# Fillers of a sparse-attention stage: a second pair of tiles for rope, another order, another share per slot

## The chip, the cores and the metric

The kernel runs on one core of a Trainium2 chip. The time is the device time of one execution in microseconds (us). Before the change the median of three runs is 815.24 us, the lowest 814.93, the highest 816.38. In the rows of the profile PE is TensorE's matmuls, PEld its weight loads, DVE VectorE, ACT ScalarE, POOL GpSimd and SP SyncE, which issues most DMAs. A letter q behind an engine's name means its sequencer.

## What is computed

One layer of a decoder on 512 tokens of width 1024, all in float32. The part that matters here, from the reference, shortened:

```
proj = h @ w_in                       # u, q, kc, vc, ks, vs, kw, vw, g_nsa, g_merge
q  = apply_rope(q)                    # 16 heads of 64
k_cmp, v_cmp = compress(kc), compress(vc)
for each block of queries:
    o_c = softmax(q k_cmp) v_cmp      # compressed branch
    o_s = softmax(q k_sel) v_sel      # selected blocks; with 8 blocks all are taken
    o_w = softmax(q k_win) v_win      # window of 512, so all earlier tokens
    o   = gate0*o_c + gate1*o_s + gate2*o_w
merged = sig(ga) * (y_pool @ w_proj_pool) + sig(gb) * (y_nsa @ w_proj_nsa)
x = x + merged @ w_out
x = x + square(relu(rms(x) @ w_ff1)) @ w_ff2
```

Rope turns each half of a head's 64 numbers against the other: `x*cos + swap(x)*sin`, where swap exchanges the halves.

## The kernel before, in words

Every product of two float32 operands is made of three matmuls of rounded halves (high times high, high times low, low times high), so a weight tile is first split into `wh` (ACT, line 351) and `wl` (DVE or POOL, line 353). A projection of 128 output channels takes 24 matmuls of 128x128 by 512 (line 394).

**The stages.** First come the normalization and most projections (`P1`, line 125), up to about 182 us; then attention, up to about 390 us; then output projections and an MLP that is worked by sums of quarter matrices, up to the end. Thirteen projections are left over from the first stage and serve as **fillers** of the attention stage (`FILL2`, line 127): `gb0` to `gb7` are gate columns whose result ACT copies to `GB`, and `q3` to `q7` are queries of head pairs 3 to 7. A filler is cut into four steps of six matmuls. After the thirteen, four more steps start the projection `pn0`, so there are 56 steps.

**Attention** runs over 96 slots, twelve for each of eight head pairs (line 988). Iteration i of the loop (line 1132) emits the scores of slot i+1 (`score_pe`, two matmuls, line 1013), the transposes of slot i-4 (`turn_pe`, line 1075), mask and minimum of slot i on DVE (`smax`, line 1035), the exponential on ACT (line 1045), the weights of slot i-1 on POOL (`weight`, line 1058), the split of the transposed block on ACT and DVE (lines 1086, 1090), and each second time the product with V (line 1109). Then come one step of each side generator (`step_side`, line 1157) and the fillers' share. At slot 3 of each pair a side generator starts the compressed branch of the next pair (`cmp_scores`, line 945; its DVE instruction at line 962 subtracts a minimum from `cw`, both in SBUF). The output of a pair is put into plane p of `oT` by DVE (line 1118).

**Rope of a query** (`rope`, line 612) is a side generator too. ACT copies the projection to `rx` (618), four DMAs on SP's queue swap its quarters into `rs` (621), POOL multiplies both by cosine and sine in halves of 128x256 (626, 629), DVE adds them (634), and then `q_done` makes `Q` of it (659 to 664). There is one pair of tiles `rx`, `rs`. The count `scored["rope"]` stands at 1 while a rope is under way, to the very end, and the filler generator gives up its turn before a `q` filler as long as it does (line 897). A rope of query i also holds its last part back until `scored["pairs"]` is i-2 (line 635), since only three tiles `Q` exist.

**The share.** After slot i the count of steps that are done is to be at least `done0 + (total - done0) * (i + 1) // 102` (line 1158), where `done0` is what was done before slot 0; the loop fills until it is there or the generator gives up. For i below 5 one step more is tried (line 1161).

**What sets the order.** The program calls are emitted as above, and a scheduler then places each engine's instructions, mostly in the order of their emission; each engine works through its own queue in order. POOL and SP also issue the DMAs that add quarters of the MLP's weights in DRAM ahead of time (`add_sum`, line 273; `make_sum`, line 265), and SP the weight loads (line 235).

Of the kernel before, what the change touches and what calls it, by code (L numbers as in the profile page):

```python
# [13 lines left out]
F32 = mybir.dt.float32  # L14
# [6 lines left out]
S = 512  # L21
# [6 lines left out]
LAG, PLAG = 4, 2  # L28
# [34 lines left out]
def trunk(ctx: ExitStack, tc: tile.TileContext, A, out):  # L63
# [4 lines left out]
    def pool(name, **kw):  # L68
        return tc.tile_pool(name=name, bufs=1, reuse_waits="tile", **kw)
# [35 lines left out]
    def add_key(k):  # L105
        i = int(k[-1]) if k[-1].isdigit() else None
        if k in IN_COLS:
            add_cols(k, w_in, IN_COLS[k])
        elif k[:2] in ("wk", "wv"):
            w = A["w_c" + k[1] + "1"][0]  # L110
            add_w(k, [(w[512 * i:512 * i + 512, :].rearrange("(k p) c -> p k c", p=128), 0)])
        elif k[0] == "V":
            k0, k1 = ((0, 3), (3, 6), (6, 8))[i]
            wv = w_in[k0 * 128:k1 * 128, :].rearrange("(k p) c -> p k c", p=128)
            add_w(k, [(wv[:, :, 1920:2048], 0), (wv[:, :, 2176:2352], 128)])
        elif k == "wpool":
            add_w(k, [(w_pool.rearrange("g c d -> c g d"), 0)])
        elif k[:2] == "pp":
            add_w(k, [(w_pp[:, 256 * i:256 * i + 256].rearrange("(k p) c -> p k c", p=128), 0)])
        else:  # L120
            c0 = {"u": 0, "q": 512, "ga": 2352, "gb": 3376}[k[:-1]]
            add_cols(k, w_in, c0 + 128 * i)
# [1 line left out]
    IN_COLS = {"ck": 1536, "cv": 1664, "ks": 1792, "kw": 2048}  # L124
    P1 = ("ck ks u0 wk0 wk1 u1 wk2 u2 kw wk3 cv V0 V1 V2 wv0 u3 wv1 q0 wv2 wpool ga0 ga1 wv3 ga2 q1 "
          "ga3 ga4 ga5 q2 ga6 ga7 pp0 pp1 pp2 pp3").split()
    FILL2 = "gb0 q3 q4 q5 gb1 gb2 q6 gb3 q7 gb4 gb5 gb6 gb7".split()
    for k in P1 + FILL2:
        add_key(k)
    for j in range(8):  # L130
# [85 lines left out]
    def emit_load():  # L216
# [20 lines left out]
        if sums_after(i):  # L237
            make_sum(began)
        if i >= len(P1) + len(FILL2) + 4 and (len(begun) > 2 or begun and st["sums"] == len(jobs)):
            add_sum()  # L240
        return True

    def sums_after(i):

        if i < MLP0:
            return len(P1) + 3 <= i < len(P1) + len(FILL2) + 8
        return i % 3 == 0
# [10 lines left out]
    def make_sum(load):  # L258

        if st["sums"] < len(jobs):  # L260
            to, q, _ = jobs[st["sums"]]
            while any(q is jobs[n][0] for n in begun):
                add_sum()
            with tc.issue_after(load.ins):
                nc.sync.dma_start(to, q)
            begun.append(st["sums"])
            st["sums"] += 1

    def add_sum(behind=None):

        to, _, q = jobs[begun.popleft()]
        with tc.issue_after(behind.ins) if behind else nullcontext():
            POOL.dma_start(to, q, accum_op=ALU.add)  # L273

    part = {}
    mode = {"pool": False, "first": POOL}
# [185 lines left out]
    def fm(key, psp, post, xT=hT, sub=0, nk=8):  # L462

        wH, wL = use(key) if isinstance(key, str) else key
        ps = psp.tile([128, S], F32, tag="F", bufs=f_banks[0], name="psF")
        yield from pieces(ps, fm_products(wH, wL, xT, sub, nk))
        r = post(ps)
        if r is not None:
            next(r)
            side.append(r)  # L470
# [9 lines left out]
    oT = op.tile([128, 8, S], F32, name="oT")  # L480
    oTf = oT.rearrange("p j t -> p (j t)")
    at = ExitStack()
    ap = at.enter_context(pool("att"))
# [124 lines left out]

    scored = {"pairs": 0, "rope": 0}
    last_exp = []  # L610

    def rope(ps, scale, done, after=0):

        assert not scored["rope"]
        scored["rope"] = 1
        xr = ap.tile([128, S], F32, tag="rx", bufs=1, name="rx")
        sw = ap.tile([128, S], F32, tag="rs", bufs=1, name="rs")
        ACT.activation(xr, ps, AF.Copy, scale=scale)
        for b in range(4):
            a = b ^ 1  # L620
            nc.sync.dma_start(sw[32 * b:32 * b + 32, :], xr[32 * a:32 * a + 32, :])
        yield
        eng = POOL if mode["pool"] else DVE
        hs = [slice(0, S // 2), slice(S // 2, S)]
        for c in hs:
            eng.tensor_tensor(xr[:, c], xr[:, c], cosT[:, c], op=ALU.mult)
            yield
        for c in hs:
            eng.tensor_tensor(sw[:, c], sw[:, c], sinT[:, c], op=ALU.mult)
            yield  # L630
        yield
        for c in hs:
            yield
            DVE.tensor_tensor(xr[:, c], xr[:, c], sw[:, c], op=ALU.add)
        while scored["pairs"] < after:
            yield
        for _ in done(xr):
            yield
        scored["rope"] = 0

    def k_done(br):
        def done(k):
# [13 lines left out]
    def q_done(p):  # L656
        def done(q):
            t = ap.tile([128, 2, S], FR, tag="Q", bufs=3, name="Q")
            ACT.activation(t[0:64, 0, :], q[0:64, :], AF.Copy)
            ACT.activation(t[64:128, 1, :], q[64:128, :], AF.Copy)  # L660
            yield
            DVE.tensor_tensor(t[64:128, 0, :], q[0:64, :], t[0:64, 0, :].bitcast(F32), op=ALU.subtract)
            yield
            DVE.tensor_tensor(t[0:64, 1, :], q[64:128, :], t[64:128, 1, :].bitcast(F32), op=ALU.subtract)
            Q[p] = t
        return done

    with ExitStack() as c1:
# [184 lines left out]
        for k in P1[2:]:  # L853
            i = int(k[-1]) if k[-1].isdigit() else None
# [35 lines left out]
    with ExitStack() as c2:  # L890
        p2 = c2.enter_context(pool("p2"))
        ps2 = c2.enter_context(pool("ps2", space=PSUM))
        def fill2():
            for k in FILL2:
                i = int(k[-1])
                if k[0] == "q":
                    while scored["rope"]:
                        yield True
                    post = (lambda i: lambda ps: rope(ps, 1.0, q_done(i), i - 2))(i)
                else:  # L900
                    def post(ps, i=i):
                        ACT.activation(GB[:, i, :], ps, AF.Copy)
                yield from fm(k, ps2, post)
            free.append(True)
            split_ready()
            early[0] = use("pn0") + (ps2.tile([128, S], F32, tag="F", bufs=F_BANKS, name="psF"),)
            for k in range(7):
                while (k, 1) not in split:
                    yield True
                proj_k(early[0], k)  # L910
                if k % 2 or k == 6:
                    ahead()
                    yield
# [4 lines left out]
        def split_ready():  # L918

            while free and ready:  # L920
                p, half = ready.pop(0)
                c = slice(256 * half, 256 * half + 256)
                ACT.activation(OT[0][:, p, c], oT[:, p, c], AF.Copy)
                DVE.tensor_tensor(OT[1][:, p, c], oT[:, p, c], OT[0][:, p, c].bitcast(F32), op=ALU.subtract)
                split.add((p, half))

        def proj_k(w, k):
            mms(w[2], split_products(w[0][:, k, :], w[1][:, k, :], OT[0][:, k, :], OT[1][:, k, :]),
                first=k == 0, last=k == 7)
# [6 lines left out]
        def fill(n=1):  # L936
            for _ in range(n):
                if next(filler, True):
                    return False
                fdone[0] += 1  # L940
            return True
# [185 lines left out]
        n = len(slots)  # L1127
        total = 4 * len(FILL2) + 4
        done0 = fdone[0]
        after = deque()  # L1130
        score_pe(0)
        for i in range(n + LAG + PLAG):
            if i < n:
                p = slots[i][0]
                if i % 12 == 3 and p + 1 < NPAIR:
                    while p + 1 not in Q:
                        fill()
                        step_side()
                if i % 12 == CMP_AT and p + 1 < NPAIR:
                    side.append(cmp_scores(p + 1))  # L1140
            if i + 1 < n:
                score_pe(i + 1)
                scored["pairs"] = (i + 2) // 12
            t = i - LAG
            if 0 <= t < n:
                turn_pe(t)
                turn_hi(t)
            if i < n:
                smax(i)
                expo(i)  # L1150
            if 0 <= i - 1 < n:
                last = weight(i - 1)
            if i % 4 == 3 and len(begun) > 1:
                add_sum(last)
            if 0 <= t < n:
                turn_lo(t)
            step_side()
            want = done0 + (total - done0) * (i + 1) // (n + LAG + PLAG)
            while fdone[0] < want and fill():
                pass  # L1160
            if i < 5:
                fill()
            j = t - PLAG
            if 0 <= j < n and j % 2 == 1 and pv(j):
                o_evac(*slots[j][0:2])
# [99 lines left out]
    with ExitStack() as c3:  # L1265
        q3 = c3.enter_context(pool("q3"))
# [339 lines left out]
    for t in (2, 3):  # L1606
        n = 512 if t == 2 else 256
# [44 lines left out]
```

## Time and profile before

| what | value |
|---|---|
| median of the runs | 815.24 us |
| the profiled execution | 814.65 us |
| its span, first to last instruction | 812.9 us |
| mean granted TensorE clock | 0.994 |
| busy PE, DVE, ACT, POOL | 788.6, 627.4, 491.6, 207.8 us |

The profile is of one execution; outside its span lie 1.75 us. A matmul that is issued with pauses is drawn longer than its pitch, so a busy PE is not always a PE at its peak, and PEclk, the granted share of the TensorE clock, has to be read beside it. In a table of windows each row gives, for each engine, the busy time and, in brackets, the instructions that overlap the window.

### The profile page before, as it was taken

What the parts mean: (1) busy time and instruction counts of PE and PEld (TensorE: products, weight loads), DVE (VectorE), ACT (ScalarE), POOL (GpSimd) and SP (SyncE); (2) the same over time, 40 slices, a digit from 0 to 9 for tenths busy, and PEclk for the clock granted to TensorE, in tenths of its full rate; (3) what the DMA queues carried; (4) which work ended last, traced back from release to release, by engine and by line L of the source; (5) the groups of instructions that cost most, each with busy time, mean ns of one, the idle gap of its engine ahead of it and who ended that gap; (6) DMA issues with size and microseconds to landing.
All of it is one profiled execution on the core that took longest, in us unless ns stands there. A gap on an engine that the chain in (4) does not pass through costs nothing.

```text
span 812.9 us, 14154 instructions
## 1 busy us (share of the span) xinstructions
PE 788.6 (97%) x5163; PEld 710.2 (87%) x5163; DVE 627.4 (77%) x1217; ACT 491.6 (60%) x968; POOL 207.8 (26%) x273
## 2 busy tenths in 40 slices
PE   8999999998899999999999999999999999999996
PEld 7889878886788888888788899999999999999996
DVE  5796744539879898889664579996889688978975
ACT  6576533337777888899434466943773477347833
POOL 4000000028766867665334100111111110000000
PEclk9999999999999999999999999999999999999999
DMA  9554633357446634553964707999998997754522
GB/s 304 143 158 122 164 92 94 102 170 153 67 124 122 144 79 92 104 131 65 328 152 154 202 9 208 311 243 283 250 286 218 285 266 194 222 164 156 181 79 104
DMA packets 128752, 136.65 MB, mean 168 GB/s; under 512 B 5349, under 2 KB 117001, under 8 KB 128522
## 3 DMA queue, kind: packets, MB, share of 16 engines
q1 hardware_dynamic: 107274, 113.98, 43.5%
q0 software_dynamic: 21120, 20.97, 18.1%
q8 instruction: 41, 0.67, 0.3%
q10 hardware_dynamic: 288, 0.79, 0.3%
q14 instruction: 29, 0.24, 0.1%
HBM read 131.01 MB, written 44.04 MB: 215 GB/s over the span
## 4 chain that ended last, share of the span: by engine, by line
PE 73%; DVE 16%; ACT 6%; issue 3%; DMA 1%; POOL 1%; ACTq 0%; DVEq 0%; POOLq 0%
PE psF L394 22%; PE psB L1379 15%; PE psB L394 12%; PE psB L1498 9%; PE psO L1109 3%; PE psT L1075 3%; PE psS L1013 2%; DVE wl L308 2%; PE psV L394 2%; DVE P L1035 2%; DVE PT L1090 1%; PE psF L451 1%; ACT P L1045 1%; DVE w3l L308 1%; PE psC L714 1%
## 5 line engine op out<-in xcount | busy, mean ns | idle before, releaser
L394 PE MATMUL psF<-R,wh 128*128 128x512 f32 x512 | 166.8, 404 | 0.9 <-ACT GB L688 0.6
L306 ACT ACTIVATE wh<-raw 128x1024 fp32r<-128x1024 f32 x70 | 74.0, 1057 | 74.5 <-PE psB L1498 32.6
L351 ACT ACTIVATE wh<-raw 128x512 fp32r<-128x512 f32 (+1 forms) x100 | 60.2, 620 | 82.2 <-PE psF L394 37.4
L394 PEld LDWEIGHTS psF<-R,wh 128*128 128x128 f32 x512 | 92.5, 189 | 18.7 <-ACT GB L688 0.8
L273 POOL DMA_DIRECT2D S<-w_ff x40 | 46.3, 1158 | 233.0 <-DMA S<-w_ff 162.5
L394 PE MATMUL psF<-R,wl 128*128 128x512 f32 x256 | 101.9, 398 | 0.8 <-DVE wl L353 0.8
L1058 POOL TENSOR_SCALAR P<-P,sm,GT 128x128 f32<-128x128 f32 (+3 forms) x128 | 85.7, 702 | 47.9 <-DVE sm L1055 34.1
L308 DVE TENSOR_TENSOR wl<-raw,wh 128x1024 fp32r<-128x1024 f32 x70 | 85.3, 1220 | 16.0 <-ACT wh L306 15.9
L353 DVE TENSOR_TENSOR wl<-raw,wh 128x512 fp32r<-128x512 f32 (+1 forms) x74 | 53.5, 734 | 32.9 <-ACT wh L351 32.5
L1045 ACT ACTIVATE P<-P,sm 128x128 f32<-128x128 f32 (+3 forms) x128 | 71.1, 557 | 12.1 <-DVE sm L1035 10.8
L1035 DVE CUSTOM_DVE_ANT_0 P<-psS,cst 128x128 f32<-128x128 f32 (+3 forms) x128 | 59.6, 483 | 6.2 <-PE psT L1075 4.6
L1379 PE MATMUL psB<-R,wh 128*128 128x256 f32 x352 | 64.1, 282 | 0.0
L353 POOL TENSOR_TENSOR wl<-raw,wh 128x512 fp32r<-128x512 f32 x28 | 39.0, 1398 | 87.6 <-ACT wh L351 85.2
L306 ACT ACTIVATE w3h<-raw 128x1024 fp32r<-128x1024 f32 x35 | 37.0, 1057 | 39.0 <-PE psB L1498 16.5
L1090 DVE TENSOR_TENSOR PT<-psT,PT 128x512 fp32r<-128x512 f32 (+2 forms) x96 | 56.6, 594 | 4.6 <-ACT PT L1086 3.5
L1086 ACT ACTIVATE PT<-psT 128x512 fp32r<-128x512 f32 (+2 forms) x96 | 49.3, 521 | 15.8 <-PE psT L1075 15.1
L394 PEld LDWEIGHTS psF<-R,wl 128*128 128x128 f32 x256 | 48.3, 188 | 11.8 <-DVE wl L353 0.9
L1075 PE MATMUL psT<-ident,P 128*128 128x128 f32 x320 | 51.6, 276 | 6.4 <-POOL P L1058 5.0
L1075 PEld LDWEIGHTS psT<-ident,P 128*128 128x128 f32 x320 | 40.2, 142 | 17.0 <-POOL P L1058 7.8
L308 DVE TENSOR_TENSOR w3l<-raw,w3h 128x1024 fp32r<-128x1024 f32 x35 | 42.7, 1221 | 15.2 <-ACT w3h L306 15.2
L1379 PEld LDWEIGHTS psB<-R,wh 128*128 128x128 f32 x352 | 54.1, 189 | 0.3 <-DVE R L1321 0.2
L1379 PE MATMUL psB<-R,wl 128*128 128x256 f32 x176 | 49.5, 281 | 0.0
(385 smaller groups left out, 2303.6 us busy)
## 6 DMA issues: line engine op xcount, KB each, us to landing
raw<-w_ff SPq DMA_DIRECT2D x55, 512.0 KB, 5.0
S<-w_ff POOLq DMA_DIRECT2D x40, 512.0 KB, 7.5
raw<-S SPq DMA_DIRECT2D x40, 512.0 KB, 5.1
raw<-w_in SPq DMA_DIRECT2D x32, 512.0 KB, 4.0
S<-w_ff SPq DMA_DIRECT2D x30, 512.0 KB, 5.6
S<-S SPq DMA_DIRECT2D x10, 512.0 KB, 6.6
raw<-w_proj_nsa SPq DMA_DIRECT2D x8, 512.0 KB, 4.1
raw<-w_out SPq DMA_DIRECT2D x8, 512.0 KB, 4.4
```

The costliest lines, as they stand in the source:

```text
L306: ACT.activation(h, t, AF.Copy)
L308: DVE.tensor_tensor(l, t, h.bitcast(F32), op=ALU.subtract)
L351: ACT.activation(h[:, sl], t[:, sl], AF.Copy)
L353: eng.tensor_tensor(l[:, sl], t[:, sl], h[:, sl].bitcast(F32), op=ALU.subtract)
L394: PE.matmul(ps, a, b, start=first and j == 0, stop=last and j == n - 1, skip_group_check=True)
L1035: DVE.tensor_tensor_reduce(out=P[:, o:o + n].rearrange("p (a c) -> p a c", c=128), in0=s, in1=m, scale=1.0, scalar=3e38, op0=ALU.add, op1= ...
L1045: last_exp[:] = [ACT.activation(c, c, AF.Exp, bias=sm[:, 0, e:e + 1], scale=-1.0, accum_out=sm[:, 1, e:e + 1])]
L1058: r = POOL.tensor_scalar(P[:, o:o + n], P[:, o:o + n], sm[:, 2, e:e + 1], GT[:, qb, c + e:c + e + 1], op0=ALU.mult, op1=ALU.mult)
L1075: PE.transpose(pt[:, 128 * j:128 * j + 128], P[:, 128 * j:128 * j + 128], ident)
L1090: DVE.tensor_tensor(dL, src, dH.bitcast(F32), op=ALU.subtract)
L1379: PE.matmul(out, w[u][:, k, 128 * f:128 * f + 128], XB[x][v][:, k, :], **kw)
L1498: PE.matmul(out, YB[y][u][:, k, 128 * f:128 * f + 128], w[v][:, k, :], **kw)
```

## The change

Four edits. Rope gets a second pair of tiles in planes 6 and 7 of `oT`, taken by turns, and up to two ropes may be under way: `q3`, `q5` and `q7` use `oT`, `q4` and `q6` use `rx` and `rs`. The fillers' list is reordered, so that gates stand between the queries, and with it the order in which their weights are loaded. A `q` filler waits only while two ropes are under way. The share of slot i becomes one step each for the first five slots plus an even part of the rest, and the extra try is gone.

```diff
-    FILL2 = "gb0 q3 q4 q5 gb1 gb2 q6 gb3 q7 gb4 gb5 gb6 gb7".split()
+    FILL2 = "gb0 gb1 q3 gb2 q4 q5 gb3 q6 q7 gb4 gb5 gb6 gb7".split()
...
+    second = [False]
...
-        assert not scored["rope"]
-        scored["rope"] = 1
-        xr = ap.tile([128, S], F32, tag="rx", bufs=1, name="rx")
-        sw = ap.tile([128, S], F32, tag="rs", bufs=1, name="rs")
+        assert scored["rope"] < 2
+        scored["rope"] += 1
+        second[0] = mode["pool"] and not second[0]
+        if second[0]:
+            xr, sw = oT[:, 6, :], oT[:, 7, :]
+        else:
+            xr = ap.tile([128, S], F32, tag="rx", bufs=1, name="rx")
+            sw = ap.tile([128, S], F32, tag="rs", bufs=1, name="rs")
...
-        scored["rope"] = 0
+        scored["rope"] -= 1
...
-                    while scored["rope"]:
+                    while scored["rope"] > 1:
                         yield True
...
-            want = done0 + (total - done0) * (i + 1) // (n + LAG + PLAG)
+            want = done0 + min(i + 1, 5) + (total - done0 - 5) * (i + 1) // (n + LAG + PLAG)
             while fdone[0] < want and fill():
                 pass
-            if i < 5:
-                fill()
```

## The prediction

> **What bounds the kernel now.** I read the page first, then a table of windows cut at the first score matmul of each head pair.
>
> ```profile
> span 812.9 us, 14154 instructions
> PE 788.6 (97%) x5163; PEld 710.2 (87%) x5163; DVE 627.4 (77%) x1217; ACT 491.6 (60%) x968; POOL 207.8 (26%) x273
> PE   8999999998899999999999999999999999999996
> PEclk9999999999999999999999999999999999999999
> PE 73%; DVE 16%; ACT 6%; issue 3%; DMA 1%; POOL 1%; ACTq 0%; DVEq 0%; POOLq 0%
> ```
>
> The last row is the chain that ended last. TensorE bounds the whole, and all it is idle is 812.9 - 788.6 = 24.3 us. A change that moves matmuls without removing any can only win idle time, or time at a lower clock. Where that lies in attention the windows tell, one row for each pair, all engines:
>
> ```profile
> 182.30:200.30 18.00, 14.87 (x83) 11.95 (x82) 16.62 (x53) 12.26 (x39) 14.09 (x20) 0.91 0.70 161
> 200.30:225.80 25.50, 22.32 (x143) 19.60 (x141) 22.85 (x72) 19.76 (x55) 17.54 (x26) 0.93 0.45 69
> 225.80:257.10 31.30, 30.54 (x185) 26.40 (x184) 25.92 (x80) 23.37 (x61) 22.34 (x32) 1.00 0.58 143
> 257.10:281.80 24.70, 24.38 (x159) 21.44 (x158) 21.75 (x73) 21.31 (x57) 19.05 (x27) 1.00 0.59 118
> 281.80:305.60 23.80, 22.85 (x150) 19.95 (x149) 21.73 (x70) 19.70 (x53) 15.75 (x24) 1.00 0.37 90
> 305.60:330.40 24.80, 24.48 (x160) 21.14 (x159) 22.09 (x72) 20.29 (x55) 17.51 (x25) 1.00 0.49 96
> 330.40:354.70 24.30, 24.04 (x158) 21.30 (x157) 20.34 (x73) 20.30 (x56) 17.30 (x26) 1.00 0.43 109
> 354.70:375.60 20.90, 20.90 (x139) 18.52 (x138) 19.15 (x68) 20.32 (x61) 12.98 (x17) 1.00 0.52 101
> ```
>
> After the window stand its length, then busy PE, PEld, DVE, ACT and POOL, then the clock. Pairs 0 and 1 have PE idle 18.00 - 14.87 = 3.13 and 25.50 - 22.32 = 3.18 us and a clock of 0.91 and 0.93; later pairs have little idle and full clock. The eight lengths sum to 193.3 us. The same windows for the fillers' line alone (L394), pairs 0 to 4 and, after the dots, pair 7; the brackets are PE and PEld:
>
> ```profile
> 182.30:200.30 18.00, 4.94 (x13) 2.64 (x13) 0.91 0.70 161
> 200.30:225.80 25.50, 6.43 (x19) 3.44 (x19) 0.93 0.45 69
> 225.80:257.10 31.30, 17.47 (x66) 11.35 (x64) 1.00 0.58 143
> 257.10:281.80 24.70, 9.73 (x36) 6.33 (x36) 1.00 0.59 118
> 281.80:305.60 23.80, 8.47 (x32) 5.26 (x30) 1.00 0.37 90
> ...
> 354.70:375.60 20.90, 8.47 (x32) 5.27 (x30) 1.00 0.52 101
> ```
>
> The weight loads (second bracket) count the filler matmuls: 13, 19, 64, 36, 30 for pairs 0 to 4, and 30 for pair 7; in the order of the built program pairs 5 and 6 have 36 each, as pair 3. So pairs 0 and 1 have few fillers and pair 2 has a heap. The code says why: `q4` waits for the rope of `q3`, `q5` for that of `q4`, and each rope runs until the scores are far enough.
>
> What stops PE, and what it costs at the clock:
>
> ```profile
> 192.98 0.44 PE L1075 MATMUL psT<-ident,P 128*128 128x128 f32 x2 [2.16 <-POOL P L1058]
> 217.72 0.96 PE L1075 MATMUL psT<-ident,P 128*128 128x128 f32 x4 [2.47 <-POOL P L1058]
> 195.00:200.00 5.00, 4.38 (x21) 3.70 (x21) 4.43 (x17) 2.82 (x8) 3.75 (x5) 0.66 0.46 121
> 215.00:220.00 5.00, 2.44 (x12) 1.78 (x11) 4.96 (x9) 2.56 (x7) 5.00 (x8) 0.90 0.63 98
> 220.00:225.00 5.00, 5.00 (x28) 4.51 (x27) 3.66 (x14) 2.35 (x7) 1.67 (x3) 0.76 0.02 3
> 189.22 4.16 DVE L962 TENSOR_TENSOR cw<-cw,c 128x256 f32<-128x256 f32 x1
> 214.47 2.79 DVE L962 TENSOR_TENSOR cw<-cw,c 128x256 f32<-128x256 f32 x1
> 189.23 1.83 POOL L626 TENSOR_TENSOR rx<-rx,cst 128x256 f32<-128x256 f32 x2
> 190.63 1.78 POOL L629 TENSOR_TENSOR rs<-rs,cst 128x256 f32<-128x256 f32 x2
> 192.02 2.31 POOL L1058 TENSOR_SCALAR P<-P,sm,GT 128x256 f32<-128x256 f32 x3
> ```
>
> PE stands before transposes whose weights POOL has not made. POOL is late because of rope, and DVE's subtraction on line 962 is stretched while POOL runs rope (189.2 to 193.4), so the next slots come late too. Behind each pause the clock dips: 5 x 0.34 = 1.7 us lost at 195 to 200, and 5 x (0.10 + 0.24) = 1.7 us at 215 to 225.
>
> **The pitch of a filler matmul**, from a stretch with nothing else on PE, for L394:
>
> ```profile
> 145.00:165.00 20.00, 20.00 (x89) 16.48 (x88) 1.00 0.42 118
> ```
>
> That is 20.00 / 89 = 0.225 us; between pairs 2 and 3 it is (31.30 - 24.70) / (64 - 36) = 0.236. I take 0.23. Six matmuls, one step, are 1.4 us.
>
> **The change part by part.** The four edits have one effect together: where the 56 steps stand. I read it from the built program's instruction order. 18 filler matmuls more come before the first score, and pairs 0 to 7 then hold 54, 30, 24, 30, 30, 24, 30 and 24, for 13, 19, 64, 36, 30, 36, 36 and 30. Both sum to 264 with the 18 counted. Work added: none; the last scores have the same work behind them.
>
> - Ahead of the first score: PE is full there (as in 145 to 165), so 18 x 0.23 = 4.1 us.
> - Pair 0: 18.0 less idle 3.1 and clock 1.7 is 13.2; 41 matmuls more are 9.4; 22.6 us.
> - Pair 1: 25.5 less 3.2 and 1.7 is 20.6, plus 11 x 0.23 = 2.5: 23.1. Pair 4, with the same 30 fillers, takes 23.8. I take 23.5.
> - Pairs 2 to 7 get lighter on PE while DVE, ACT and POOL keep their work. DVE is busy 21.73 of 23.80 us in pair 4, so a lighter pair may not get shorter at all. The bounds are the full pitch and nothing. Pair 2 with 24, from pair 4: 22.4 to 23.8, I take 23.1. Pair 3 with 30: 23.3 to 24.7, 24.0. Pair 4: 23.8. Pair 5 with 24: 22.0 to 24.8, 23.4. Pair 6 with 30: 22.9 to 24.3, 23.6. Pair 7 with 24: 19.5 to 20.9, 20.2. I take the middles, since PE and DVE are about equally near in these rows.
>
> The sum is 4.1 + 22.6 + 23.5 + 23.1 + 24.0 + 23.8 + 23.4 + 23.6 + 20.2 = 188.3 us for 193.3 before, so 5.0 us less. With the lower ends (pair 1 at 23.1) it is 183.7, 9.6 less; with the upper ends (pair 1 at 23.8) 192.8, 0.5 less.
>
> The second pair of tiles costs nothing itself: the same ACT copy, four DMAs, four POOL and two DVE instructions for each rope, on other addresses. Planes 6 and 7 of `oT` are first written with results at slot 81, long after `q7`'s rope (slots 53 to 63 in the order of emission), and in the built program the writes of `oT` wait for ACT alone. On SP's queue the swap of `q3` now stands behind a copy that waits for an addition which POOL issues:
>
> ```profile
> 183.23 2.45 SPq L621 DMA_DIRECT2D rs<-rx  x4
> 188.34 1.26 POOL L273 DMA_DIRECT2D S<-w_ff  x1
> 194.69 0.49 SPq L265 DMA_DIRECT2D S<-S  x1
> ```
>
> Before, the addition went out at 188.3 and the copy at 194.7, 6.4 us later. In the new order POOL's addition stands ahead of its first work for attention, so its landing should be past before `q3` is projected; I count 0, and up to 6.4 us on rope, not on PE, if not. Preparing the fillers' weights (lines 351, 353) moves into pair 0, where DVE has 18.00 - 16.62 us free and the pair gets longer: 0.
>
> An added wait: in DVE's queue both additions of `q3`'s rope (line 634) now stand ahead of line 962 and of the next slots' `smax`, and they wait for POOL and the swap. ACT's exponentials and PE's transposes of slots 5 and on are behind it. PE then has six fillers in nearly each slot, and the transposes lag four slots, so I count 0 in the forecast and price it as a rival.
>
> **What the Trainium skill says.** On "SBUF — State Buffer", in "Who interferes with whom", it states that a VectorE instruction with two SBUF inputs and a GpSimd instruction that reads SBUF exclude each other, and that whoever starts first holds the port for its whole instruction. The row of 4.16 us outlasts four rope instructions of POOL, so here the wait was more than one of them. By the page a meeting would cost at most one POOL instruction, and the rival below would lose its price. On "TensorE: Matmul & The Clock Gate", in "What's actually happening", the clock falls after an idle window of about 3.4 us. No pause here is so long, yet the dips stand right behind pauses of 2.16 and 2.47 us. By the page the 3.4 us of lost clock might have another cause and stay: the sum would be 1.6 us less than before instead of 5.0.
>
> **The rivals.**
>
> (a) *Slower: rope holds DVE in the new places.* Its price is what a meeting cost in pairs 0 and 1, idle and clock: 3.1 + 1.7 = 4.8 and 3.2 + 1.7 = 4.9 us. The forecast takes both away; one that comes back leaves 815.24 - 5.0 + 4.9 = 815.1, two give 820.0, so it decides from the second of five ropes on. For it: the queue order above, and DVE with no more than 2 us free in a pair. Against it: a meeting in pair 4 had little effect, with fillers at hand.
>
> ```profile
> 284.21 1.55 DVE L634 TENSOR_TENSOR rx<-rx,rs 128x256 f32<-128x256 f32 x1
> 286.65 0.39 DVE L634 TENSOR_TENSOR rx<-rx,rs 128x256 f32<-128x256 f32 x1
> ```
>
> There 1.55 for 0.39 us on DVE cost pair 4 at most its idle 23.80 - 22.85 = 0.95.
>
> (b) *No change: DVE is the floor.* Then the lighter pairs keep their lengths: 0.5 us less, 814.7. For it speaks DVE's 21.73 of 23.80; against it that pair 4, with 30 fillers, is shorter than pairs 3 and 5 with 36. To the same end comes an attention that is shorter while the MLP then waits for its weights.
>
> (c) *More: the full pitch.* 9.6 us less, 805.6. For it: PE is named on the chain, and is busy 24.38 of 24.70 in pair 3.
>
> That the fillers are not spread after all can be left out, since the built order shows them.
>
> **How the numbers follow.** The profiled execution took 814.65 us and would take 809.65; the median of the runs lies 0.6 above, so I predict 815.24 - 5.0 = 810.2 us. Chances: the forecast, anywhere from 1.6 to about 9 us less, 0.62; (c) 0.06; (b) 0.12; (a) 0.20. Of 815 us 0.2% is 1.6 us, about what a measurement of this kernel can tell from no change. So faster 0.68, same 0.12, slower 0.20. The forecast's own range is 806 to 813.6. The range for 8 in 10 reaches from 805.6, the lower bound, to 817.5, which takes in (b) and the milder part of (a).
>
> **What would show it.** In the changed profile: the first score at about 186.5; pair 0 at 22 to 23 us with full clock; no transpose that waits more than 1 us for POOL in pairs 0 and 1; line 962 near 0.4 to 0.6 us; pair 2 near 23; the others 23 to 24, and PE idle in each no more than 1.5 us. It is wrong if PEclk dips after 186, if pairs 2 to 6 stay above 24.3 (then DVE is the floor), or if the swap of `q3` goes out late.

## The result, and the profile after

The changed kernel is slower: 820.91 us median of 4 runs (819.66 to 821.23), against 815.09 for the kernel before on the same chip, a ratio of 1.0067 with a 95% interval of 1.0049 to 1.0084. The forecast was 810.2. The profiled execution took 819.66 us. In its rows the lines of attention stand five further down than before: rope's multiplications (626, 629) are 631 and 634 and its additions (634) are 639, the compressed branch (957, 958, 962) is 962, 963 and 967, 1013 is 1018, 1035 is 1040, 1058 is 1063, 1075 is 1080, 1090 is 1095, 924 is 929.

From the page of the changed kernel, the span, the busy times and the chain:

```profile
span 817.9 us, 14160 instructions
...
PE 788.4 (96%) x5163; PEld 709.3 (87%) x5163; DVE 620.2 (76%) x1217; ACT 489.8 (60%) x968; POOL 209.6 (26%) x273
...
PE 67%; DVE 13%; ACT 9%; DMA 5%; issue 4%; POOL 2%; SPq 1%; ACTq 0%; POOLq 0%; DVEq 0%
```

The work is the same (788.4 for 788.6 us of PE), the span is 5.0 us longer, and in the chain PE has 6 points less and DVE 3, while ACT and DMA have 7 more. The windows by head pair, cut as before:

```profile
186.20:213.70 27.50, 24.27 (x126) 20.00 (x125) 18.30 (x60) 16.31 (x47) 17.35 (x25) 0.94 0.68 162
213.70:240.20 26.50, 23.14 (x152) 20.04 (x151) 22.88 (x73) 19.83 (x55) 19.92 (x27) 1.00 0.61 110
240.20:262.30 22.10, 21.58 (x145) 18.46 (x144) 20.35 (x71) 19.22 (x53) 18.18 (x25) 1.00 0.55 108
262.30:286.90 24.60, 22.88 (x153) 20.17 (x152) 20.40 (x72) 20.11 (x56) 16.93 (x24) 1.00 0.49 119
286.90:312.30 25.40, 22.99 (x153) 20.32 (x152) 23.47 (x77) 20.88 (x56) 20.52 (x30) 1.00 0.34 74
312.30:334.00 21.70, 21.16 (x144) 18.71 (x144) 19.03 (x68) 18.36 (x52) 15.55 (x22) 1.00 0.44 87
334.00:356.60 22.60, 22.58 (x152) 20.00 (x151) 18.96 (x69) 19.28 (x55) 15.32 (x24) 1.00 0.39 82
356.60:377.00 20.40, 19.86 (x134) 17.46 (x133) 19.02 (x66) 19.65 (x59) 12.38 (x17) 1.00 0.35 78
sum 190.80, PE 178.46 PEld 155.16 DVE 162.41 ACT 153.64 POOL 136.16; mean PE 22.31 PEld 19.40 DVE 20.30 ACT 19.20 POOL 17.02
```

The first score stands at 186.2, as forecast. Pairs 0 and 1, which were to take 22.6 and 23.5 us, take 27.5 and 26.5, and still have PE idle 27.50 - 24.27 = 3.23 and 26.50 - 23.14 = 3.36 us. The other pairs are at most 0.6 us above the forecast, or below it, but for pair 4 (25.40 for 23.8). What holds pairs 0 and 1, from the timeline of the changed kernel (DVE, then POOL, then PE; start, duration, and in brackets the idle time before and what ended it):

```profile
198.14 2.80 DVE L639 TENSOR_TENSOR oT<-oT 128x256 f32<-128x256 f32 x1 [2.73 <-POOL oT L634]
200.87 0.41 DVE L963 TENSOR_TENSOR cw<-psC,cw 128x256 f32<-128x256 f32 x1
...
226.86 2.23 DVE L639 TENSOR_TENSOR rx<-rx,rs 128x256 f32<-128x256 f32 x1 [2.07 <-POOL rs L634]
...
195.55 1.87 POOL L631 TENSOR_TENSOR oT<-oT,cst 128x256 f32<-128x256 f32 x2
196.94 1.85 POOL L634 TENSOR_TENSOR oT<-oT,cst 128x256 f32<-128x256 f32 x2
198.36 1.05 POOL L1063 TENSOR_SCALAR P<-P,sm,GT 128x384 f32<-128x384 f32 x1
198.99 1.66 POOL L353 TENSOR_TENSOR wl<-raw,wh 128x512 fp32r<-128x512 f32 x1
...
201.43 0.47 PE L1018 MATMUL psS<-KH,Q 128*128 128x512 f32 x1 [1.25 <-DVE cw L963]
203.50 0.63 PE L1080 MATMUL psT<-ident,P 128*128 128x128 f32 x4 [1.37 <-DVE PT L1095]
```

DVE reaches rope's first addition at 195.4, stands 2.73 us until POOL has made its input, and then needs 2.80 us for an instruction of 0.41, until POOL comes to a gap at 200.65. So DVE does nothing for 5.1 us, and what stands behind in its queue waits: line 963, which empties one of the buffers that the score matmuls write into, and the masks of slots 5 and on. PE has fillers up to 200 and then works 1.87 us of the next five, and the clock falls behind it:

```profile
200.00:205.00 5.00, 1.87 (x9) 0.99 (x8) 4.83 (x14) 1.59 (x5) 1.32 (x2) 0.99 0.30 67
205.00:210.00 5.00, 4.90 (x22) 4.37 (x23) 3.24 (x12) 2.90 (x8) 4.01 (x6) 0.67 0.74 180
```

There is a second loss behind the last score (the tail). The timeline of the changed kernel again:

```profile
380.55 2.52 DVE L929 TENSOR_TENSOR R<-oT,R 128x256 fp32r<-128x256 f32 x4
...
383.59 0.68 DVE L1040 CUSTOM_DVE_ANT_0 P<-psS,cst 128x512 f32<-128x512 f32 x1
...
399.51 1.19 PE L394 MATMUL psB<-R,wh 128*128 128x512 f32 x2 [2.81 <-ACT mH L1282]
```

and the same last matmul of this stretch in the kernel before:

```profile
395.61 0.70 PE L394 MATMUL psB<-R,wh 128*128 128x512 f32 x2 [1.67 <-ACT mH L1279]
```

The mask of the last slot, whose score was made at 377.0, comes at 383.6, behind six pieces of the split of finished planes of `oT` (line 929, `x2` at 379.27 and the `x4` above). From the last score to the first `psB` it is 399.5 - 377.0 = 22.5 us, for 395.6 - 375.6 = 20.0 before. And the pause of 2.81 us is followed by a low clock, which the 1.67 us of before are not. First the window of the changed kernel:

```profile
399.50:402.00 2.50, 2.49 (x6) 2.02 (x7) 2.40 (x4) 0.63 (x1) 0.40 (x1) 0.50 1.00 277
402.00:406.00 4.00, 4.00 (x16) 3.20 (x16) 0.44 (x1) 0.00 (x0) 1.15 (x1) 0.89 1.05 391
```

then that of the kernel before:

```profile
395.60:398.10 2.50, 2.50 (x11) 2.05 (x12) 2.50 (x3) 1.14 (x2) 1.58 (x1) 1.00 1.04 369
```

That is 2.5 x 0.50 + 4.0 x 0.11 = 1.7 us more. The account against the forecast for this execution, 819.66 - 809.65 = 10.0 us: pairs 190.8 - 184.2 = 6.6; first score 0.2 early; the stretch behind the last score 2.5; the rest of the span (817.9 - 399.5 = 418.4 for 812.9 - 395.6 = 417.3) 1.1, in which the 1.7 of clock lie. The sum is 10.0.

### The profile page after: what moved, and what is told of

Same layout as the page of the kernel before. It is cut to its first block, busy times and chain, and to the rows that moved or that the text cites. A ratio compares the mean times of both kernels' runs of the same rounds, so it can differ in the third digit from the quotient of the medians.

```text
span 817.9 us, 14160 instructions
## 1 busy us (share of the span) xinstructions
PE 788.4 (96%) x5163; PEld 709.3 (87%) x5163; DVE 620.2 (76%) x1217; ACT 489.8 (60%) x968; POOL 209.6 (26%) x273
## 4 chain that ended last, share of the span: by engine, by line
PE 67%; DVE 13%; ACT 9%; DMA 5%; issue 4%; POOL 2%; SPq 1%; ACTq 0%; POOLq 0%; DVEq 0%
PE psF L394 20%; PE psB L1382 14%; PE psB L394 12%; PE psB L1501 9%; ACT P L1050 2%; PE psO L1114 2%; DVE wl L308 2%; PE psT L1080 2%; PE psV L394 2%; PE psS L1018 2%; ACT PT L1091 1%; PE psF L451 1%; DMA S<-w_ff 1%; DVE P L1040 1%; PE psC L719 1%
## 5 line engine op out<-in xcount | busy, mean ns | idle before, releaser
L1063 POOL TENSOR_SCALAR P<-P,sm,GT 128x128 f32<-128x128 f32 (+3 forms) x128 | 89.1, 737 | 49.5 <-DVE sm L1060 30.8
L1050 ACT ACTIVATE P<-P,sm 128x128 f32<-128x128 f32 (+3 forms) x128 | 71.2, 558 | 23.9 <-DVE sm L1040 23.0
L1091 ACT ACTIVATE PT<-psT 128x512 fp32r<-128x512 f32 (+2 forms) x96 | 49.1, 519 | 10.7 <-PE psT L1080 10.0
L353 POOL TENSOR_TENSOR wl<-raw,wh 128x512 fp32r<-128x512 f32 x28 | 37.3, 1337 | 52.4 <-ACT wh L351 48.2
```

What stands on the lines that cost most here:

```text
L353: eng.tensor_tensor(l[:, sl], t[:, sl], h[:, sl].bitcast(F32), op=ALU.subtract)
L1050: last_exp[:] = [ACT.activation(c, c, AF.Exp, bias=sm[:, 0, e:e + 1], scale=-1.0, accum_out=sm[:, 1, e:e + 1])]
L1063: r = POOL.tensor_scalar(P[:, o:o + n], P[:, o:o + n], sm[:, 2, e:e + 1], GT[:, qb, c + e:c + e + 1], op0=ALU.mult, op1=ALU.mult)
L1091: ACT.activation(dH, src, AF.Copy)
```

## The experiments

**Theory 1**: rope's work on POOL holds DVE's queue in pairs 0 and 1, by the wait for its result and by what POOL does to a DVE instruction with two inputs in SBUF. **Theory 2**: the tail is late since the split of `oT` stands ahead of the last mask. Rivals: the pairs are long because 54 and 30 filler matmuls stand there; DVE is full; the second rope under way, the list or the share costs it. Each kernel was timed beside the kernel before on one chip; before's medians were 815.04 for runs 1 to 4, 814.39 for 5 to 8 and 815.07 for 9 to 12.

**1. Rope's additions later in DVE's queue.** Line 639 is tied behind the newest mask (`last_min` holds the newest instruction of line 1040).

```diff
-            DVE.tensor_tensor(xr[:, c], xr[:, c], sw[:, c], op=ALU.add)
+            with behind(last_min[0]) if last_min[0] else nullcontext(): DVE.tensor_tensor(xr[:, c], xr[:, c], sw[:, c], op=ALU.add)
```

> The changed kernel, and only the two additions of rope (line 639) tied to stand in DVE's queue behind the newest slot's mask and minimum (line 1040), so behind slots 8 and 9 instead of ahead of slot 5. Every instruction is kept, and the same fillers stand in the same pairs. Theory 1 (DVE stands at the first addition until POOL has made rope, and the slots behind it come late): the time over the forecast of pairs 0 and 1, 27.5 - 22.6 = 4.9 and 26.5 - 23.5 = 3.0 us, goes; with 820.9 before this edit that is about 813. Theory 2 (POOL holds any instruction of DVE with two inputs in SBUF, so the stall only moves to the next one, line 967, which now stands ahead of slot 5): line 967 takes 2 to 4 us in place of 0.4, the wait of 2.7 us is saved at most once or twice, 816 to 820. Theory 3 (the pairs are long since 54 and 30 filler matmuls with their weight splits stand there, whatever the order): no change, 820 to 821.5.

Measured: 813.23 us (811.4 to 814.74), ratio 0.9973 [0.9959, 0.9988]. The windows of this kernel, pairs 0 and 1 and the sum of all eight, and its DVE timeline:

```profile
186.30:211.40 25.10, 22.64 (x126) 18.79 (x125) 20.30 (x59) 16.38 (x46) 16.68 (x24) 1.00 0.74 176
211.40:235.30 23.90, 23.25 (x151) 19.98 (x150) 23.01 (x74) 19.92 (x55) 20.20 (x28) 1.00 0.67 120
...
sum 183.40, PE 177.40 PEld 154.09 DVE 165.34 ACT 153.56 POOL 136.78; mean PE 22.18 PEld 19.26 DVE 20.67 ACT 19.20 POOL 17.10
...
196.19 4.78 DVE L967 TENSOR_TENSOR cw<-cw,c 128x256 f32<-128x256 f32 x1
```

With the same fillers in the same pairs the eight pairs take 183.4 us, near the forecast's 184.2, so the third theory falls: the matmuls were not the cause. The time is theory 1's. Of the 7.4 us that the pairs get shorter, pair 0 has 2.4 and pair 1 has 2.6; pairs 3 and 4 have 2.3. In pair 3 of the changed kernel there was a third, smaller wait at line 639 (DVE stands 2.12 us for POOL up to 284.86, and PE 1.12 us behind it), which goes too. But theory 2 of this expectation is also seen: line 967 now takes 4.78 us, up to 200.97, where POOL's chain (the same as above, 194.5 to 200.7) ends. What was saved is not the stall itself but what stood behind it: line 963 ran at 195.3 in place of 200.87, the score of the next slot had its buffer, and the clock stayed at 1.00. Pair 0 still has 2.5 us more than forecast.

**2. The split not before slot 95.**

```diff
-            want = done0 + min(i + 1, 5) + (total - done0 - 5) * (i + 1) // (n + LAG + PLAG)
+            want = (as above) if i >= n - 1 else min(52, (as above))
```

> The changed kernel, and only the last steps of the share held back: the step that lets the finished planes of oT be split (lines 928, 929) is not taken before slot 95, as in the kernel before, where it follows that slot's mask (line 1040). Tail theory (in the changed kernel the split of 14 pieces stands ahead of slot 95's mask on DVE, whose score is at 377.0 and whose mask is at 383.6): about 3.5 us less than 820.9, so 817 to 818, and pairs 0 to 6 unchanged. Rival (the tail waits for something else, weights or the MLP's additions, and the gain is lost at a later wait): 820 to 821.

Measured: 817.79 us (816.01 to 820.1), ratio 1.0031 [1.0017, 1.0044]: 3.1 us less than 820.91. The timeline of this kernel, and the window behind its first `psB`:

```profile
379.90 0.69 DVE L1040 CUSTOM_DVE_ANT_0 P<-psS,cst 128x512 f32<-128x512 f32 x1
...
398.87 0.47 PE L394 MATMUL psB<-R,wh 128*128 128x512 f32 x1 [1.67 <-ACT mH L1282]
...
398.80:401.30 2.50, 2.43 (x11) 2.01 (x12) 2.50 (x3) 1.20 (x3) 1.58 (x1) 1.00 1.13 283
```

The last score is at 377.7 here, so the stretch is 21.2 us for 22.5, and with the pause back at 1.67 us the clock holds: 1.3 and 1.7 us, which is the gain.

**3. The edits of runs 1 and 2 together.**

> Both edits together, rope's additions behind the newest slot's mask and the split not before slot 95. If theory 1 and the tail theory hold and add up: 820.9 - 7.9 - 3.5 = 809.5, faster than the kernel before by 0.7%. If theory 2 and the tail theory hold: 812 to 817. If the pairs are long whatever the order: 817.

Measured: 811.37 us (809.57 to 812.61), ratio 0.9948 [0.9931, 0.9964]. The two gains, 7.7 and 3.1, add up to 10.8 and give 9.5 together, faster than the kernel before by 0.5%.

**4. The kernel before with the split one slot earlier.**

```diff
-            want = done0 + (total - done0) * (i + 1) // (n + LAG + PLAG)
+            want = done0 + (total - done0) * (i + 1) // (n + LAG + PLAG) if i != n - 2 else 53
```

> The kernel before, and only the 53rd step of the share taken one slot earlier, at slot 94, so that the split of oT (line 924) stands ahead of slot 95's mask (line 1035) as in the changed kernel. Tail theory: 3 to 4 us more than before, 818 to 819. Rival (the tail of the changed kernel comes from the order of the fillers or of the weights' loads): within 0.5 us of before.

Measured: 815.7 us (814.55 to 816.88), ratio 1.0006 [0.9994, 1.0017], so 0.5 less to 1.4 us more; the expected 3 to 4 us were too many, and the times alone do not tell a small loss from none. The timeline of this kernel:

```profile
380.96 0.68 DVE L1035 CUSTOM_DVE_ANT_0 P<-psS,cst 128x512 f32<-128x512 f32 x1
...
396.94 0.70 PE L394 MATMUL psB<-R,wh 128*128 128x512 f32 x2 [1.89 <-ACT mH L1279]
```

The mask is late as in the changed kernel, and the stretch grows from 20.0 to 396.9 - 375.6 = 21.3 us, the same 1.3 as in run 2. But the pause is 1.89 us, and no low clock follows (1.00 from 396.9 to 399.4). So by the traces the place of the split costs 1.3 us in either kernel, and 1.7 more where the pause grows to 2.8.

**5. The edits of runs 1 and 2, and line 967 two slots later.**

```diff
-            yield
-            DVE.tensor_tensor(wf, wf, s8[:, 0, :, None]...
+            for _ in range(3 if p else 1): yield
+            with behind(last_min[0]) if last_min[0] else nullcontext(): DVE.tensor_tensor(wf, wf, s8[:, 0, :, None]...
```

> The changed kernel with both edits of before (rope's additions behind the newest slot's mask, the split of oT not before slot 95), and line 967 (the compressed branch's subtraction, two inputs in SBUF) two slots later, at slot 8 for slot 5. In the run with the additions alone moved, line 967 took 4.78 us, from 196.19 to the end of a chain of POOL instructions without a gap. The next DVE instruction in the queue with two inputs in SBUF is now the weight split of line 353, just ahead of slot 5's mask. If POOL's unbroken run holds whichever such instruction comes first: line 353 takes 4 to 5 us in place of 0.7, pair 0 stays near 25 us, and the time stays at 811 to 812. If it is line 967 itself, or its place: pair 0 falls to 22.6 to 23.5 and the time to 808.5 to 809.5.

Measured: 810.46 us (808.46 to 812.07), ratio 0.9944 [0.9928, 0.9959]. The DVE timeline of this kernel:

```profile
197.14 4.55 DVE L353 TENSOR_TENSOR wl<-raw,wh 128x512 fp32r<-128x512 f32 x1 [0.49 <-ACT wh L351]
```

The stall went to the next instruction with two inputs in SBUF, as the first theory of this expectation had it: 4.55 us for 0.68, and pair 0 takes 24.7 us. The time lies between the two ranges. It is no matter of one line: here POOL's chain held whichever came first.

**6. Rope's multiplications on DVE.** This takes the chain away and gives DVE more work.

```diff
-        eng = POOL if mode["pool"] else DVE
+        eng = DVE
```

> The changed kernel, and only rope's four multiplications by cosine and sine on VectorE in place of POOL, in the five ropes of attention. The same fillers stand in the same pairs. DVE gets 20 instructions of about 0.41 us more, 8.2 us in all, POOL loses 20 of 0.7 to 1.2. If the loss is that rope on POOL holds DVE (by the wait for its result, or by the port): no instruction of DVE takes over 2 us in pairs 0 and 1, and the time falls from 820.9 to 812 to 816, in spite of more work on DVE. If DVE is simply too full in these pairs: slower than 820.9, up to 829.

Measured: 811.04 us (808.57 to 812.06), ratio 0.995 [0.9935, 0.9965], 9.9 us less than the changed kernel. Windows of this kernel, pairs 0 and 1 and the sum of all eight:

```profile
186.00:208.20 22.20, 22.20 (x125) 19.02 (x124) 17.78 (x64) 16.53 (x47) 15.20 (x21) 1.00 0.83 200
208.20:232.20 24.00, 22.91 (x152) 20.07 (x151) 21.64 (x77) 19.88 (x55) 16.19 (x22) 1.00 0.63 114
...
sum 182.10, PE 178.20 PEld 154.43 DVE 166.83 ACT 153.64 POOL 122.94; mean PE 22.27 PEld 19.30 DVE 20.85 ACT 19.20 POOL 15.37
```

DVE has 166.83 - 162.41 = 4.4 us more to do in these pairs and the pairs are 8.7 us shorter. No DVE instruction takes over 1.4 us in pairs 0 and 1. Pair 0, with its 54 filler matmuls, has no idle PE at all and takes 22.2 us, for 22.6 in the forecast.

**7. The kernel before with line 962 two slots later** (the edit of run 5 there).

> The kernel before, and only line 962 (the subtraction with two inputs in SBUF, 4.16 and 2.79 us in pairs 0 and 1 of before) two slots later and behind that slot's mask. It keeps before's fillers, 12, 19 and 65 in the first three pairs. If the pauses of pairs 0 and 1 in the kernel before come from DVE being held at that line: its time there is below 1 us, and 2 to 6 us of the 9.7 that these pairs lose by idle and clock go, 809 to 813. If they come from POOL being late with the weights, or from too few fillers, as the forecast had it: within 1 us of 815.0.

Measured: 816.34 us (815.13 to 817.68), ratio 1.0022 [1.0013, 1.003]. This is 1.1 to 2.4 us more than before, outside both expectations. Windows of pairs 0 and 1, and the timeline of DVE and PE, of this kernel:

```profile
182.40:200.00 17.60, 14.71 (x83) 12.26 (x82) 13.25 (x50) 12.23 (x39) 13.84 (x20) 0.90 0.73 168
200.00:222.20 22.20, 20.97 (x142) 18.08 (x140) 21.22 (x72) 19.59 (x55) 17.85 (x26) 1.00 0.49 75
...
191.86 1.96 DVE L634 TENSOR_TENSOR rx<-rx,rs 128x256 f32<-128x256 f32 x2 [1.86 <-POOL rs L629]
...
195.84 0.54 DVE L962 TENSOR_TENSOR cw<-cw,c 128x256 f32<-128x256 f32 x1
...
193.08 0.44 PE L1075 MATMUL psT<-ident,P 128*128 128x128 f32 x2 [2.28 <-POOL P L1058]
```

The stretch of line 962 is gone (0.54 for 4.16 us). Pair 1 gains 25.5 - 22.2 = 3.3 us and loses its dip of the clock. Pair 1 of before was thus held by line 962. Pair 0 keeps its pause, 2.28 us before a transpose whose weights POOL makes behind rope, and on DVE the stall has only moved: rope's two additions, now ahead of line 962, stand 1.86 us for POOL and then take 1.96 us. In pair 4 the first of them stands 1.45 and takes 2.35 us, and pairs 2 and 4 get 1.2 and 2.0 us longer. So this run does not tell POOL's rope from a lack of fillers in pair 0; run 10 does.

**8. The changed kernel with one rope at a time.**

```diff
-                    while scored["rope"] > 1:
+                    while scored["rope"]:
```

> The changed kernel, and only the old condition back: a query's filler waits while one rope is under way. The new order of the list and the new share stay. The fillers then stand 34, 26, 42, 26, 40, 24 and 30 in pairs 0 to 6. The additions of q3's rope still stand ahead of slot 5's mask, those of q4's at slots 20 and 21 in place of 17. By the theory of the wait at rope's additions: pair 0 keeps its loss of about 5 us and pair 1 loses its 3 us, 817 to 819. If the second rope under way, or its tiles in oT, cost it: 813 to 815.

Measured: 825.01 us (824.76 to 827.25), ratio 1.0137 [1.0121, 1.0154], slower still, so the second rope under way is not what costs. Nor are its tiles in `oT`, which runs 6 and 12 keep. Window of pair 0, DVE and PE of this kernel:

```profile
185.60:210.50 24.90, 20.65 (x106) 17.70 (x104) 15.64 (x53) 14.34 (x42) 14.22 (x20) 0.86 0.63 160
...
197.45 2.78 DVE L639 TENSOR_TENSOR oT<-oT 128x256 f32<-128x256 f32 x1 [2.75 <-POOL oT L634]
...
200.71 0.77 PE L1018 MATMUL psS<-KH,Q 128*128 128x512 f32 x1 [4.01 <-DVE cw L963]
...
226.74 3.07 DVE L967 TENSOR_TENSOR cw<-cw,c 128x256 f32<-128x256 f32 x1
```

The same meeting as in the changed kernel, and with 34 filler matmuls in place of 54 PE stands 4.01 us for 1.25. Pair 1 does not get free either: now line 967 meets the next rope (3.07 us), and the pair takes 27.0 us with 26 filler matmuls. My 817 to 819 counted one meeting at one price; there were two, and that of pair 0 cost PE more with fewer fillers beside it.

**9. Rope on DVE and the split not before slot 95** (the edits of runs 6 and 2).

> The changed kernel with rope's multiplications on VectorE in place of POOL, and the split of oT not before slot 95. With rope alone on VectorE it was 811.0, pair 0 took 22.2 us with 54 filler matmuls, and the stretch behind the last score still had 7.6 us of idle PE. If the loss of the tail is of its own, 2.5 to 3.5 us more go: 807.5 to 808.5, the fastest so far. If the tail only waits for what the MLP needs: 810 to 811.

Measured: 809.08 us (807.84 to 809.98), ratio 0.9924 [0.9911, 0.9937], the lowest median of all (its interval overlaps that of run 5), 6.0 us below the kernel before, and between the two expectations. The tail's loss is of its own: of the 3.1 us of run 2 some 2.0 come again here.

**10. The kernel before with rope on DVE** (the edit of run 6 there).

> The kernel before, and only rope's multiplications of attention on VectorE in place of POOL; the fillers stand 19, 25, 52, 36, 30, 36 and 36 in pairs 0 to 6, heaped as before. If it is the spread fillers that win time once rope is off POOL: 813 to 815, since pairs 0 and 1 still lack fillers. If rope on VectorE alone is the win, and the spread is worth nothing: 807 to 810.

Measured: 811.83 us (810.51 to 813.83), ratio 0.9962 [0.9949, 0.9975], between the two expectations. Windows of pairs 0 and 1 of this kernel:

```profile
181.90:196.70 14.80, 14.48 (x89) 12.14 (x88) 13.84 (x56) 12.15 (x39) 11.33 (x15) 1.00 0.75 185
196.70:219.40 22.70, 22.61 (x149) 18.98 (x147) 22.19 (x76) 19.95 (x54) 16.65 (x23) 1.00 0.57 82
```

With 19 and 25 filler matmuls, six more in each pair than before and fewer than in the changed kernel, PE is idle 0.32 and 0.09 us, for 3.13 and 3.18 before, and the clock is full. So the pauses of pairs 0 and 1 in the kernel before came with rope on POOL, and no even spread was needed to end them. Part of the gain is lost in pairs 2 and 5, where PE is idle 2.9 and 2.2 us. Of the 6.0 us of run 9, 3.2 are had without any change to the fillers, and 2.8 come from the change with its split mended.

**11. The changed kernel with the old share** (the last part of the change undone).

```diff
-            want = done0 + min(i + 1, 5) + (total - done0 - 5) * (i + 1) // (n + LAG + PLAG)
+            want = done0 + (total - done0) * (i + 1) // (n + LAG + PLAG)
...
+            if i < 5:
+                fill()
```

> The changed kernel, and only the share and the extra try of before back. The fillers then stand 31, 29, 30, 30, 36, 30 and 30 in pairs 0 to 6, more evenly than in the changed kernel; the additions of q3's rope still stand near slot 5's mask, those of q4's fall to slot 26, and the split of oT comes at slot 95 again. By the theory of the wait: one meeting in pair 0 with few fillers beside it (5 to 8 us in the run with one rope under way), none in pair 1, and the tail's 3 us saved: 815 to 818. If it is the 18 matmuls more in pair 0 that cost the time: 810 to 813.

Measured: 817.62 us (814.17 to 820.85), ratio 1.0031 [1.0017, 1.0045], as the theory of the wait had it. DVE in this kernel:

```profile
195.28 4.90 DVE L967 TENSOR_TENSOR cw<-cw,c 128x256 f32<-128x256 f32 x1
```

One meeting in pair 0, on line 967 this time, and none in pair 1, where PE is idle 0.11 of 24.8 us. The stretch behind the last score is 21.0 us, with a pause of 1.89 us in place of 2.81.

**12. The changed kernel with the old list.**

```diff
-    FILL2 = "gb0 gb1 q3 gb2 q4 q5 gb3 q6 q7 gb4 gb5 gb6 gb7".split()
+    FILL2 = "gb0 q3 q4 q5 gb1 gb2 q6 gb3 q7 gb4 gb5 gb6 gb7".split()
```

> The changed kernel, and only the old order of the list back (gb0 q3 q4 q5 gb1 ...). The fillers stand 15, 63, 30, 30, 30, 24 and 30 in pairs 0 to 6; the additions of q3's rope stand at slots 2 and 5, those of q4's at 9 and 10, those of q5's at 17. By the theory of the wait: two ropes meet DVE's queue in pair 0 with few fillers beside them, and one in pair 1: no better than the changed kernel, 820 to 826. If the reordered list is what costs: 814 to 817.

Measured: 813.14 us (812.8 to 814.24), ratio 0.998 [0.9971, 0.9988]: 7.8 us less than the changed kernel and below both expectations (820 to 826, 814 to 817). Windows, DVE and POOL of this kernel:

```profile
186.60:204.10 17.50, 14.19 (x87) 11.59 (x86) 15.20 (x53) 12.72 (x39) 16.17 (x24) 1.00 0.48 108
...
sum 183.70, PE 177.34 PEld 154.33 DVE 162.01 ACT 154.59 POOL 135.34; mean PE 22.17 PEld 19.29 DVE 20.25 ACT 19.32 POOL 16.92
...
195.35 2.62 DVE L967 TENSOR_TENSOR cw<-cw,c 128x256 f32<-128x256 f32 x1
...
187.47 1.44 POOL L631 TENSOR_TENSOR oT<-oT,cst 128x256 f32<-128x256 f32 x2 [2.30 <-DMA oT<-oT]
```

I had counted the additions ahead of the masks and not looked where POOL's chain falls. Here `q3`'s rope is on POOL at 187.47, at the first slots, and the next rope's meeting is short, 2.62 us. Pair 0 has as few fillers as before (15 matmuls) and pair 1 a heap of 63, and yet the eight pairs take 183.7 us, as little as with the spread fillers of run 1. So the reordered list is the edit that did the harm; that it did so by putting `q3`'s rope beside slots 4 and 5 is read from the two timelines. An even spread is not needed to reach the forecast's sum. The tail is as late as in the changed kernel (22.5 us, with a pause of 2.81 us); this list with the split held back was not run.

## Why the prediction was wrong

The pair lengths, from the tables of windows, in us (in all but before, 3.7 to 4.3 us more stand ahead of the first score):

| pair | before | forecast | after | additions later | rope on DVE | old list |
|---|---|---|---|---|---|---|
| 0 | 18.0 | 22.6 | 27.5 | 25.1 | 22.2 | 17.5 |
| 1 | 25.5 | 23.5 | 26.5 | 23.9 | 24.0 | 31.2 |
| 2 to 7 | 149.8 | 138.1 | 136.8 | 134.4 | 135.9 | 135.0 |
| sum | 193.3 | 184.2 | 190.8 | 183.4 | 182.1 | 183.7 |

- **The first step that failed is the added wait**: "PE then has six fillers in nearly each slot, and the transposes lag four slots, so I count 0 in the forecast and price it as a rival." The fillers lasted until 200; DVE was held from 195.4 to 200.9, and behind it stood not the transposes alone but line 963, which empties a buffer of the score matmuls. Pairs 0 and 1 came out 4.9 and 3.0 us above the forecast. Moving the additions wins 7.7 us in the medians (run 1, 5.0 of them in these pairs), taking rope off POOL 9.9 (run 6). The row of 4.16 us that I took for a stretch of line 962 was already this: it is not the line, it is POOL's chain, and with line 962 moved away the next instruction took its place in pair 0 (run 7).
- **The second is the tail**: "Work added: none; the last scores have the same work behind them." The work is the same, its order is not: the share reaches the step that starts the split one slot earlier, and the split stands ahead of the last mask. 1.3 us of stretch and 1.7 us of clock, 3.1 in the medians (run 2). I read the order of the fillers from the built program and not that of DVE behind the last score. Of the 2.5 us of that stretch 1.2 remain in run 2; their cause stays open.
- Rival (a) was the right mechanism, with two large meetings as it counted and a smaller third. Its 820.0 hits the time partly by luck: of the 10.7 us above the forecast the meetings gave some 7.7, and the tail, which (a) does not name, some 3.
- Right were the first score at 186.2, line 967 at 0.4 to 1.0 us (0.4 to 0.6 in the forecast), the swap of `q3` in time, and, once the meetings are gone, the pair lengths: 22.2 and 24.0 for 22.6 and 23.5, 135.9 for 138.1 (run 6). Rival (b), DVE as the floor, is refuted: pairs 2, 5, 6 came out 1.0 to 1.7 us below the forecast.
- That pairs 0 and 1 of before lost time because they lacked fillers was at best half right. With rope off POOL they have next to no idle PE at 19 and 25 filler matmuls (run 10), and pair 1 gains 3.3 us at its old 19 when line 962 moves (run 7).
- On the Trainium skill's page "SBUF — State Buffer", "Who interferes with whom", which lets whoever starts first keep the port for its instruction: the exclusion is borne out, since only DVE instructions with two inputs in SBUF were held (lines 639, 967, 353) and line 963, with one from PSUM, never. The price of one POOL instruction, which the prediction drew from it, is not: 4.78, 4.55 and 4.90 us are each several POOL instructions.
- On the Trainium skill's page "TensorE: Matmul & The Clock Gate", "What's actually happening", with its idle window of about 3.4 us: here the clock fell to 0.50 behind a pause of 2.81 us, to 0.57 in run 1 and 0.78 in run 6 behind pauses of 2.81 and 2.82, and stayed at 1.00 behind 1.67 and 1.89, so a shorter pause was enough.

## What to carry to other kernels

Before a wait is priced at nothing, list all that stands behind it in the same queue, the instruction that empties a score buffer among it, and see how long the waiter's own input takes to be made. When an instruction with two SBUF inputs is long in a trace, look at what POOL does in that time, and move or shorten POOL's chain; moving the long instruction can merely pass the stall on, as in runs 1, 5 and 7. A change of how fillers are shared also moves whatever the last filler sets off, so read the order at the end of the stage too.

## What the runs showed of the hardware

A DVE instruction with two SBUF inputs that met a chain of POOL instructions without gaps waited for several of them, not for one: 4.78 us beside six in run 1 (196.19 to 200.97, where POOL's last ended at 200.68), 4.55 and 4.90 us in runs 5 and 11. It did not always wait for the chain's end: in run 12 the one of 2.62 us ended at 197.97, while POOL worked on without a gap to 202. What decides when DVE gets in was not tried by itself. With 20 rope instructions moved from POOL to DVE the kernel got faster, though DVE was the second busiest engine.
